# Zero-padded query blocks as stationary operand of the low-part score products in a forgetting attention

## The chip, the cores and the metric

The kernel runs on one core of one Trainium2 chip as a single launch. The metric is the device time of that core in microseconds (us). A profiled execution leaves a trace, whose times count from the first instruction of the span. TensorE (PE) multiplies matrices and has a queue of its own for loading stationary operands (PEld); VectorE is DVE, ScalarE is ACT, GpSimd is POOL, and SyncE (SP) issues DMAs.

## The reference

Two transformer blocks run one after the other on a sequence of 1024 tokens of width 1024, all in float32. The change touches only the attention of the first block, which has 8 heads of dimension 64:

```
logit[t,s] = q_t . k_s / sqrt(64) + c[t] - c[s]      c = cumsum(log_sigmoid(f)),  s <= t
p = softmax(logit);   out = p @ v
```

It is swept in blocks of 128 queries, so a head has 8 query blocks, and block i needs (i+1)*128 keys. Around it stand a gated spatial unit, the output projection and a gated feed-forward layer; the second block has a windowed attention of 16 heads, a convolution and 16 experts.

## The kernel before

**Precision.** TensorE takes fp32r operands. To come close to float32, each operand is split into a high part (the value rounded to fp32r) and a low part (the rest), and a product is the sum of high*high, high*low and low*high. A head has only 64 rows to contract, so for its scores two of these products share one matmul: `stack_q` (line 575) writes for each head a tile of 128 partitions in which one half holds the high part of q and the other half its low part. For the even head of a pair the high part is in partitions 0 to 63, for the odd head in 64 to 127. `stack_k` (line 590) writes for each head a tile with the high part of k in both halves. One matmul over 128 partitions then gives high*high plus low*high. The third product, high q with low k, is a second matmul. The low parts of both heads of a pair share one tile `kl`, even head in partitions 0 to 63 and odd head in 64 to 127, so this second matmul contracts over 64 partitions only (line 688).

**The steps.** `steps` (line 664) lists the 64 pairs (head, query block). In the steady part they come in the order (m-1,3), (m-1,2), (m,7), (m,6), (m-1,1), (m-1,0), (m,5), (m,4). Blocks 4 to 7 are the big ones. A big step's scores fill a PSUM tile `sb` of two banks, a small one's a tile `ss` of one bank; there is one buffer of each (`psp`, line 639).

**The stages of a step.** `score_mm` (S) makes the scores: per chunk of up to 512 keys the stacked product (L685), on the diagonal block also an identity times the causal mask (L687), and the low product (L688). `score_max` (M, L698, DVE) adds the keys' c, scales and takes the maximum. `score_exp` (E, L706, ACT) makes the exponentials. `probs_T` (T, L721, PE) transposes them in 128x128 blocks. `probs_H` (H, L727, ACT) and `probs_L` (L, L731, DVE) split them into high and low parts. `pvmm` (V, L740 and L741, PE) multiplies with v for two steps at once; `pv_out` (O) adds the two halves of its result, on DVE (L752) or on POOL (L756). `pair_sum` and `pair_mul` (L764, L771, L773) apply the softmax sums.

**The order** is written by hand. Every engine runs its queue in program order. `ORDB` (line 638) lists what iteration n of the main loop (line 802) emits and with what delay: V(n-6), L(n-4), T(n-3), O(n-6), the pair's normalisation, S(n), H(n-3), M(n), E(n-1). So on PE an iteration is V, T, S; on DVE L, O, M; on ACT O, H, E; on POOL the additions of O and the copies of `pair_sum`.

**The second block's attention** makes its scores with `score_mm2` (lines 1402 to 1415). It has the same stacked queries, but its low keys `kl` carry zeros in partitions 64 to 127 (L1322), so all four of its score matmuls contract over 128 partitions.

Of the kernel before, what the change touches and what calls it, by code (L numbers as in the profile page):

```python
# [9 lines left out]
F32R = mybir.dt.float32r  # L10
# [8 lines left out]
P = 128  # L19
# [3 lines left out]
def fused(tc, x, mix_norm_g, w_in, b_f, sgu_ln_g, sgu_ln_b, w_s, b_s, out_norm_g, w_out,  # L23
# [13 lines left out]
    ACT, DVE, POOL, PE = nc.scalar, nc.vector, nc.gpsimd, nc.tensor  # L37
    act = nc.scalar.activation
    ES = ExitStack()
    L, R = "left", "right"  # L40

    def pool(es, name, bufs=1, side=L, space=None):
        kw = dict(name=name, bufs=bufs)
        if space is not None:
            kw["space"] = space
        else:
            kw["side"] = side
        return es.enter_context(tc.tile_pool(**kw))
# [4 lines left out]
    def rd(ap):  # L53
        return ap.bitcast(F32)

    def split(h, l, src, scale=None):
        if scale is None:
            act(h, src, AF.Copy)  # L58
            DVE.tensor_tensor(l, src, rd(h), op=OP.subtract)  # L59
        else:  # L60
            act(h, src, AF.Copy, scale=scale)
            DVE.scalar_tensor_tensor(l, src, scale, rd(h), op0=OP.mult, op1=OP.subtract)
# [101 lines left out]
    def wsrc(w, k0, kc, c0, n):  # L164
        return w[k0 * P:(k0 + kc) * P, c0:c0 + n].rearrange("(k p) n -> p k n", p=P)
# [151 lines left out]
    for src in (mix_norm_g, out_norm_g, ffn_norm_g, norm1_g_2, norm2_g_2, conv_w_2, b_mod_2, c_2, c_ctx_2):  # L317
        n = 1
# [166 lines left out]
    for g4 in range(2):  # L485
# [3 lines left out]
        o = slice(g4 * 4, g4 * 4 + 4)  # L489
# [84 lines left out]
    qk = []  # L574
# [60 lines left out]
    es_b = ExitStack()  # L635
# [4 lines left out]
    pst = pool(es_b, "pst", 4, space=PSUM)  # L640
    ps1 = pool(es_b, "ps1", 1, space=PSUM)
    pvs = pool(es_b, "pvs", 2, R)
    pol = pool(es_b, "pol", 3, R)
    psm = pool(es_b, "psm", 3, R)
    ppt = pool(es_b, "ppt", 2, R)
    ptn = pool(es_b, "ptn", 2, R)
# [5 lines left out]
    def prep(j):  # L652
        vs[j] = pvs.tile([P, NT, 2, P], F32R, name="vhl")
        h, l = vs[j][:, :, :, :64], vs[j][:, :, :, 64:]
        vv = vraw[:, :, j * P:(j + 1) * P].rearrange("p t (o d) -> p t o d", o=2)
        for o in range(2):
            if 2 * j + o not in cns:
                cn_load(2 * j + o)
        return [
            lambda: act(h, vv, AF.Copy),  # L660
            lambda: DVE.tensor_tensor(l, vv, rd(h), op=OP.subtract),
        ]

    steps = []
# [5 lines left out]
                steps += [(m, 7 - a), (m, 6 - a)]  # L670
    live, half, pts = {}, {}, {}

    def score_mm(n):
        h, i = steps[n]
        q, k, l = qk[h]
        r = slice(64 * (h % 2), 64 * (h % 2) + 64)
        nk = (i + 1) * P
        blk = slice(i * P, i * P + P)
        if i > 3:
            sp = psp.tile([P, T], F32, name="sb", bufs=1)  # L680
        else:
            sp = psp.tile([P, 512], F32, name="ss", bufs=1)
        for c0 in range(0, nk, 512):
            cs = slice(c0, min(c0 + 512, nk))
            PE.matmul(sp[:, cs], q[:, blk], k[:, cs], start=True, stop=False)  # L685
            if c0 + 512 >= nk:
                PE.matmul(sp[:, blk], idR, cmR, start=False, stop=False)  # L687
            PE.matmul(sp[:, cs], q[r, blk], l[r, cs], start=False, stop=True)  # L688
        live[n] = sp

    def score_max(n):
# [85 lines left out]
    def done(n, d):  # L777
        h, i = steps[n]
        if i == 0 and h % 2 and h < 7:
            for x, f in zip((FS[0], last + FS[1], last + FS[2], last + FS[3]),  # L780
                            (lambda j: pair_sum(j, 0), lambda j: pair_mul(j, 0), lambda j: pair_sum(j, 1), lambda j: pair_mul(j, 1))):
                if d == x:
                    f(h // 2)
        if (h, i) == (7, 0) and d == dict(ORDB)["E"] + 1:
            DVE.reciprocal(rinv, tns[3][:, 1].rearrange("p i o -> p (i o)"))
            rx[3] = sq.rearrange("p (i o d) -> p i (o d)", o=2, d=64)
            todo.append(lambda: DVE.tensor_copy(rx[3].rearrange("p i (o d) -> p (i o) d", o=2),
                                                rinv[:, :, None].to_broadcast([P, 16, 64])))
# [7 lines left out]
    def stage(f, n):  # L796
        if 0 <= n < N:
            f(n)

    ASQ = max(steps.index((5, 0)) + last + FS[3], steps.index((7, 7))) + 1  # L800
    table = dict(S=score_mm, M=score_max, E=score_exp, T=probs_T, H=probs_H, L=probs_L, V=even(pvmm), O=even(pv_out))
    for n in range(N + last + 1):
        if n < N and steps[n] in ((0, 7), (2, 7), (4, 7), (6, 7)):
            oT.append((pq if oT else po0).tile([P, T], F32, name="qk"))
        for c, d in ORDB:
            if c == "F":
                for d in range(last + 8):
                    stage(lambda m: done(m, d), n - d)
            else:
                stage(table[c], n - d)  # L810
        if n < N and steps[n][1] == 5 and steps[n][0] in (1, 3, 5):
            todo.extend(prep(steps[n][0] // 2 + 1))
        if n < N and steps[n] == (6, 7):

            r4, r5, rw, h4, l4, wh0, wl0 = [pq.tile([P, T], F32 if i < 3 else F32R, name="qk") for i in range(7)]
            k2 = lambda a: a[:, :768].rearrange("p (k n) -> p k n", k=2)
            nc.sync.dma_start(r4, d_sgu[0])
            nc.sync.dma_start(k2(rw), wsrc(w_out, 4, 2, 0, 384))
            nc.sync.dma_start(r5, d_sgu[1])
            todo.extend([lambda: split(h4, l4, r4), lambda: split(k2(wh0), k2(wl0), k2(rw))])  # L820
        if n < N and steps[n] == (7, 7):
            h5, l5, sqs, sq = [pq.tile([P, T], F32R if i < 2 else F32, name="qk") for i in range(4)]
            todo.append(lambda: split(h5, l5, r5))

            def attn_sq(j):
                act(sq if j else sqs, oT[j], AF.Square)
                if j:
                    POOL.tensor_tensor(sqs, sqs, sq, op=OP.add)

            todo.extend([lambda j=j: attn_sq(j) for j in range(2)])  # L830
        if n == ASQ:
            todo.append(lambda: attn_sq(2))
        if todo and n >= 2:
            todo.popleft()()
# [17 lines left out]
    for i in range(NPART):  # L852
        n = -(-(FF - f0) // (NPART - i))
# [53 lines left out]
    for k in (6, 7):  # L907
# [4 lines left out]
                stage=2, scols=1536, pcols=768, name="w2")  # L912
# [456 lines left out]
    es_b = ExitStack()  # L1369
# [408 lines left out]
    for r in range(P // 8):  # L1778
        o = slice(8 * r, 8 * r + 8)
# [123 lines left out]
    for t in range(NT + 2):  # L1903
# [10 lines left out]
        if u >= 0:  # L1914
            r = rso[:, u:u + 1]
# [66 lines left out]
```

## Time and profile before

| | |
|---|---|
| runs (us) | 3078.14, 3086.30, 3086.57 |
| median (us) | 3086.3 |
| profiled execution (us) | 3078.3 |
| its span (us) | 3076.5 |
| mean granted TensorE clock, of full speed | 0.982 |
| PE busy | 2946.9 us, 96% of the span |
| DVE busy | 1730.7 us, 56% |
| ACT busy | 1350.4 us, 44% |
| POOL busy | 350.8 us, 11% |

The first block's attention runs from 254 to 414 us of the span, the second block's from 1920 to 2218 us. The ends of matmuls are modelled in the trace, and a matmul's duration overlaps the next one's. What a matmul takes of TensorE's time is therefore read from one start to the next, not from its duration.

### The profile page before, as it was taken

What the parts mean: (1) busy time and instruction counts of PE and PEld (TensorE: products, weight loads), DVE (VectorE), ACT (ScalarE), POOL (GpSimd) and SP (SyncE); (2) the same over time, 40 slices, a digit from 0 to 9 for tenths busy, and PEclk for the clock granted to TensorE, in tenths of its full rate; (3) what the DMA queues carried; (4) which work ended last, traced back from release to release, by engine and by line L of the source; (5) the groups of instructions that cost most, each with busy time, mean ns of one, the idle gap of its engine ahead of it and who ended that gap; (6) DMA issues with size and microseconds to landing.
All of it is one profiled execution on the core that took longest, in us unless ns stands there. A gap on an engine that the chain in (4) does not pass through costs nothing.

```text
span 3076.5 us, 36785 instructions
## 1 busy us (share of the span) xinstructions
PE 2946.9 (96%) x14183; PEld 2442.4 (79%) x14183; DVE 1730.7 (56%) x2485; ACT 1350.4 (44%) x2107; POOL 350.8 (11%) x301
## 2 busy tenths in 40 slices
PE   9999999999999999999999999788899879999996
PEld 7987778888888888788888888677778768888885
DVE  4345763645354445833311123787842479999998
ACT  5345753212111212422121111788821368888886
POOL 2200122000000001200000012111121301111112
PEclk9999999999999999999999999999999889999998
DMA  5120140323222222321122221000153589999997
GB/s 195 44 74 14 40 139 26 108 72 98 67 99 84 92 79 65 126 60 42 55 69 76 89 83 35 1 21 15 44 199 136 178 304 368 377 371 378 377 377 278
DMA packets 287903, 411.88 MB, mean 134 GB/s; under 512 B 13244, under 2 KB 141984, under 8 KB 287728
## 3 DMA queue, kind: packets, MB, share of 16 engines
q1 hardware_dynamic: 275744, 371.34, 34.9%
q0 software_dynamic: 10496, 37.14, 3.9%
q8 instruction: 111, 1.82, 0.3%
q10 hardware_dynamic: 1488, 1.06, 0.2%
q14 instruction: 64, 0.52, 0.1%
HBM read 365.94 MB, written 43.55 MB: 133 GB/s over the span
## 4 chain that ended last, share of the span: by engine, by line
PE 82%; DVE 6%; ACT 5%; issue 3%; DMA 3%; POOL 1%; SPq 0%; POOLq 0%; DVEq 0%; ACTq 0%
PE b L65 24%; PE b L67 24%; PE b L66 24%; ACT sm L1432 1%; ACT ph L1454 1%; PE pt L721 1%; PE b L1823 1%; PE sb L688 1%; PE po L740 1%; DVE wl L59 1%; DVE pl L1462 1%; PE sb L685 1%; PE po L741 1%; DVE sm L1425 1%; PE pt L1444 0%
## 5 line engine op out<-in xcount | busy, mean ns | idle before, releaser
L59 DVE TENSOR_TENSOR wl<-wst,wh 128x1024 fp32r<-128x1024 f32 (+2 forms) x560 | 661.4, 1211 | 452.1 <-ACT wh L58 444.2
L58 ACT ACTIVATE wh<-wst 128x1024 fp32r<-128x1024 f32 (+2 forms) x560 | 578.3, 1044 | 379.7 <-PE b L66 161.1
L66 PE MATMUL b<-xn,wh 128*128 128x512 f32 x1312 | 510.7, 389 | 2.2 <-POOL xn L1185 1.3
L65 PE MATMUL b<-xn,wh 128*128 128x512 f32 x1312 | 511.7, 390 | 0.2 <-ACT xn L1187 0.2
L67 PE MATMUL b<-xn,wl 128*128 128x512 f32 x1312 | 510.8, 389 | 0.5 <-DVE wl L59 0.5
L65 PE MATMUL b<-wh,a 128*128 128x512 f32 x768 | 302.4, 394 | 0.2 <-ACT a L58 0.2
L66 PE MATMUL b<-wl,a 128*128 128x512 f32 x768 | 299.9, 390 | 0.8 <-DVE wl L59 0.8
L67 PE MATMUL b<-wh,a 128*128 128x512 f32 x768 | 299.7, 390 | 0.4 <-DVE a L59 0.4
L66 PEld LDWEIGHTS b<-xn,wh 128*128 128x128 f32 x1312 | 246.4, 188 | 53.8 <-POOL xn L1185 1.7
L67 PEld LDWEIGHTS b<-xn,wl 128*128 128x128 f32 x1312 | 246.3, 188 | 52.3 <-DVE wl L59 1.1
L65 PEld LDWEIGHTS b<-xn,wh 128*128 128x128 f32 x1312 | 246.3, 188 | 51.4 <-ACT xn L1187 0.6
L67 PEld LDWEIGHTS b<-wh,a 128*128 128x128 f32 x768 | 144.6, 188 | 31.0 <-DVE a L59 1.1
L66 PEld LDWEIGHTS b<-wl,a 128*128 128x128 f32 x768 | 144.7, 188 | 30.5 <-DVE wl L59 1.6
L65 PEld LDWEIGHTS b<-wh,a 128*128 128x128 f32 x768 | 144.8, 188 | 29.6 <-ACT a L58 0.7
L65 PE MATMUL b<-hH,wh 128*128 128x512 f32 x352 | 137.7, 391 | 0.0
L67 PE MATMUL b<-hH,wl 128*128 128x512 f32 x352 | 137.1, 389 | 0.0
L66 PE MATMUL b<-hL,wh 128*128 128x512 f32 x352 | 136.9, 389 | 0.0
L1462 DVE TENSOR_TENSOR pl<-pt,ph 128x512 fp32r<-128x512 f32 x152 | 102.1, 687 | 32.5 <-ACT ph L1454 31.5
L1865 POOL DMA_INDIRECT d_x<-b,idxT x15 | 65.8, 4387 | 469.8 <-DVE b L1859 469.8
L58 ACT ACTIVATE hH<-sg 128x512 fp32r<-128x512 f32 x44 | 27.8, 632 | 202.7 <-DVE sg L1049 202.7
L1425 DVE CUSTOM_DVE_ANT_0 sm<-sp,mk,nsk 128x640 f32<-128x640 f32 (+1 forms) x128 | 107.1, 838 | 3.8 <-PE sp L1414 2.4
L1042 ACT ACTIVATE sg<-sg 128x512 f32<-128x512 f32 x44 | 27.7, 633 | 179.6 <-DVE sg L1041 179.6
(511 smaller groups left out, 5501.7 us busy)
## 6 DMA issues: line engine op xcount, KB each, us to landing
wst<-in_w_exp_gate_dram SPq DMA_DIRECT2D x128, 512.0 KB, 10.8
wst<-in_w_exp_up_dram SPq DMA_DIRECT2D x128, 512.0 KB, 10.8
wst<-in_w_exp_down_dram SPq DMA_DIRECT2D x128, 512.0 KB, 11.1
wst<-in_w_in_dram SPq DMA_DIRECT2D x74, 512.0 KB, 3.9
mw<-in_w_mod_dram SPq DMA_DIRECT2D x48, 512.0 KB, 4.8
wst<-in_w_gate_up_dram SPq DMA_DIRECT2D x44, 512.0 KB, 4.1
wst<-in_w_down_dram SPq DMA_DIRECT2D x16, 512.0 KB, 3.8
wst<-in_w_out_dram SPq DMA_DIRECT2D x10, 512.0 KB, 4.0
```

What stands on the lines that cost most here:

```text
L58: act(h, src, AF.Copy)
L59: DVE.tensor_tensor(l, src, rd(h), op=OP.subtract)
L65: PE.matmul(ps, lh, rh, start=start, stop=False)
L66: PE.matmul(ps, lh, rl, start=False, stop=False)
L67: PE.matmul(ps, ll, rh, start=False, stop=stop)
L685: PE.matmul(sp[:, cs], q[:, blk], k[:, cs], start=True, stop=False)
L688: PE.matmul(sp[:, cs], q[r, blk], l[r, cs], start=False, stop=True)
L721: PE.transpose(pt[:, b * P:(b + 1) * P], sm[:, (k0 + b) * P:(k0 + b + 1) * P], ident)
L740: PE.matmul(po[:, c:], v, ph[:, kb, c:], start=kb == 0, stop=False)
L1425: DVE.tensor_tensor_reduce(sms[n][:, :nk], sps.pop(n)[:, 256:256 + nk], (mk if i else mk0)[:, :nk], -0.125, nsk[:, hd:hd + 1], op0=OP.add, ...
L1462: DVE.tensor_tensor(pl, pt, rd(ph), op=OP.subtract)
L1865: nc.gpsimd.indirect_dma_start(out=d_x2, out_offset=bass.IndirectOffsetOnAxis(ap=idxT[:, e:e + 1], axis=0), in_=y, in_offset=None, compute ...
```

## The change

For the low product a stationary tile of 128 partitions is made, which has the high part of the query block in the head's own 64 partitions and zeros in the other 64. There are four such tiles, by head parity and block parity. POOL zeroes their other halves once ahead of the main loop, and copies a step's query block into the head's half two steps ahead of its use (`pad_q`, emitted right behind `score_mm` in the loop). The low product then takes the padded tile against all 128 partitions of `kl`; the other head's low keys meet zeros. The pool `pol`, from which O takes its tiles `ol`, has two buffers in place of three.

```diff
-    pol = pool(es_b, "pol", 3, R)
+    pol = pool(es_b, "pol", 2, R)
...
+    pqz = pool(es_b, "pqz", 1, R)
+    qzs = [[pqz.tile([P, P], F32R, name=f"qz{c}") for c in range(2)], [pqz.tile([P, P], F32R, name=f"qz{2 + c}") for c in range(2)]]
+    for o in range(2):
+        for t in qzs[o]:
+            POOL.memset(rd(t[64 - 64 * o:128 - 64 * o, :]), 0.0)
+    pads = {}
+
+    def pad_q(n):
+        h, i = steps[n]
+        r = slice(64 * (h % 2), 64 * (h % 2) + 64)
+        qz = qzs[h % 2][i % 2]
+        POOL.tensor_copy(qz[r, :], rd(qk[h][0][r, i * P:i * P + P]))
+        pads[n] = qz
+
+    pad_q(0)
+    pad_q(1)
+
     def score_mm(n):
         h, i = steps[n]
         q, k, l = qk[h]
-        r = slice(64 * (h % 2), 64 * (h % 2) + 64)
+        qz = pads.pop(n)
...
             PE.matmul(sp[:, cs], q[:, blk], k[:, cs], start=True, stop=False)
             if c0 + 512 >= nk:
                 PE.matmul(sp[:, blk], idR, cmR, start=False, stop=False)
-            PE.matmul(sp[:, cs], q[r, blk], l[r, cs], start=False, stop=True)
+            PE.matmul(sp[:, cs], qz, l[:, cs], start=False, stop=True)
...
             else:
                 stage(table[c], n - d)
+            if c == "S":
+                stage(pad_q, n + 2)
```

## Rows read from the trace of the kernel before

**Rows 1.** Chain of waits from 254 to 414 us: what ended last, by line.
```profile
by line: PE pt L721 23.5%; PE sb L688 14.5%; PE po L740 14.0%; PE sb L685 12.0%; PE po L741 11.4%; PE ss L688 7.0%; PE ss L685 3.3%; DVE sb L698 3.0%; issue 2.6%; PE pt L771 1.6%; PE ss L687 1.5%; PE sb L687 1.4%; DVE lb L731 1.2%; ACT qk L
```
**Rows 2.** Windows: length, busy time and count by engine, granted clock, DMA share, GB/s.
```profile
254.00:274.00 20.00, 15.68 (x49) 10.19 (x47) 9.79 (x18) 10.23 (x19) 0.00 (x0) 0.66 0.00 0
274.00:407.00 133.00, 131.93 (x804) 101.27 (x802) 99.59 (x234) 105.31 (x253) 20.16 (x27) 1.00 0.09 32
```
**Rows 3.** TensorE in order of time, first attention: start us, duration us, engine, line.
```profile
321.23 0.98 PE L721 MATMUL pt<-ident,sb 128*128 128x128 f32 x7
321.97 0.47 PE L685 MATMUL sb<-qk 128*128 128x512 f32 x1
322.37 0.50 PE L688 MATMUL sb<-qk 64*128 64x512 f32 x1
322.80 0.39 PE L685 MATMUL sb<-qk 128*128 128x256 f32 x1
323.02 0.22 PE L687 MATMUL sb<-cmR,idR 128*128 128x128 f32 x1
323.18 0.38 PE L688 MATMUL sb<-qk 64*128 64x256 f32 x1
323.49 0.38 PE L740 MATMUL po<-hs,vhl 128*128 128x256 f32 x1
323.71 0.28 PE L741 MATMUL po<-ls,vhl 128*128 128x256 f32 x1
323.83 0.28 PE L740 MATMUL po<-hs,vhl 128*128 128x256 f32 x1
...
324.30 0.22 PE L740 MATMUL po<-hs,vhl 128*128 128x128 f32 x1
324.36 0.28 PE L741 MATMUL po<-ls,vhl 128*128 128x128 f32 x1
```
**Rows 4.** The same view in the second block's attention.
```profile
2100.40 0.48 PE L1474 MATMUL po<-ph,vhl 128*128 128x512 f32 x1
2100.72 0.40 PE L1475 MATMUL po<-pl,vhl 128*128 128x512 f32 x1
2100.95 0.28 PE L1411 MATMUL sp<-kh,qs 128*128 128x256 f32 x1
2101.07 0.28 PE L1412 MATMUL sp<-kl,qs 128*128 128x256 f32 x1
2101.19 0.34 PE L1413 MATMUL sp<-kh,qs 128*128 128x384 f32 x1
```
**Rows 5.** Windows in the second block's attention; columns as in Rows 2.
```profile
2000.00:2200.00 200.00, 172.94 (x1085) 147.21 (x1084) 161.09 (x339) 177.26 (x408) 25.45 (x33) 0.97 0.05 17
2006.00:2008.00 2.00, 0.69 (x5) 0.45 (x4) 2.00 (x5) 1.94 (x6) 0.22 (x1) 0.93 0.00 0
2008.00:2010.00 2.00, 2.00 (x7) 1.71 (x8) 1.29 (x3) 1.95 (x5) 0.51 (x1) 0.50 0.03 8
```
**Rows 6.** DVE in order of time: the maxima of three big steps.
```profile
257.99 1.22 DVE L698 CUSTOM_DVE_ANT_0 sb<-sb,wst 128x1024 f32<-128x1024 f32 x1
...
333.31 1.22 DVE L698 CUSTOM_DVE_ANT_0 sb<-sb,wst 128x1024 f32<-128x1024 f32 x1 [0.87 <-issue]
...
342.48 0.96 DVE L698 CUSTOM_DVE_ANT_0 sb<-sb,wst 128x768 f32<-128x768 f32 x1 [0.76 <-PE sb L688]
```
**Rows 7.** POOL's groups: busy us, mean ns, idle before by releaser.
```profile
L756 POOL TENSOR_TENSOR qk<-qk,ol 64x256 f32<-64x256 f32 x14 | 11.7, 834 | 173.4 <-ACT ol L755 164.0 <-ACT hs L727 9.4
...
L1322 POOL MEMSET kl<- 64x1280 f32 x2 | 2.3, 1162 | 0.1
...
L611 POOL CAST idR<-ident 128x128 fp32r<-128x128 f32 x1 | 0.3, 301 | 0.0
```
**Rows 8.** TensorE in order of time at the first attention's start.
```profile
254.16 0.40 PE L67 MATMUL b<-xtH,wl 128*128 128x512 f32 x1
...
254.73 0.50 PE L688 MATMUL sb<-qk 64*128 64x512 f32 x1
...
259.27 0.49 PE L685 MATMUL sb<-qk 128*128 128x512 f32 x1 [3.13 <-DVE tn L698]
```

## The prediction

> **What bounds the kernel now.** I first read the chain of waits over the first block's attention, 254 to 414 us of the span [rows 1]: the chain lies on TensorE, and the low score product, L688, holds 14.5% and 7.0% of it, 34 of 160 us. The windows say the same [rows 2]: from 274 to 407 us PE is busy 131.93 of 133 us at full clock, ACT 105.31, DVE 99.59, POOL 20.16. So in these 133 us TensorE sets the pace, and ACT, the next, could end 28 us sooner. From 254 to 274 us it is different: PE is busy 15.68 of 20 us, at a granted clock of 0.66.
>
> Then I read PE in order of time, from start to start, since durations overlap [rows 3]. The reader is to see three kinds of step. Among products of 128 partitions, 256 columns take 0.12 us (L741 to L740, 323.71 to 323.83) and 128 columns take 0.06 (L740 to L741, 324.30 to 324.36); 512 columns take 0.23 (L1475 to L1411, [rows 4]). Behind the product of 64 partitions the next one starts late: 512 columns take 0.43 (322.37 to 322.80), 256 take 0.31 (323.18 to 323.49). And ahead of it too: L687 with 128 columns takes 0.16 until L688 starts (323.02 to 323.18). The second attention makes the same low product with 128 partitions, and there L1412 takes 0.12 for 256 columns, before it and behind it nothing is late [rows 4].
>
> **The change part by part.** *The low product.* There are 96 of them, 12 for each head (two chunks for each of the blocks 4 to 7, one for each of the others). Each keeps its columns; only its height changes.
> - Behind it: 0.43 - 0.23 = 0.20 at 512 columns and 0.31 - 0.12 = 0.19 at 256. 96 x 0.20 = 19.2 us.
> - Ahead of it: in 64 cases L687 stands there, 0.16 - 0.06 = 0.10; I take 0.09, as the trace has 0.14 to 0.16, so 5.8 us. In 32 it is a 512-column L685, which takes 0.40 (321.97 to 322.37) in place of 0.23. But that L685 follows transposes, and in the second attention the first product behind transposes takes 0.32 (L1474, 2100.40 to 2100.72) without any change of height. So 0.09 of it stays, and 32 x 0.08 = 2.6 us go.
> - One product further on: the first one behind L688 is itself slow, L740 0.22 (323.49 to 323.71) and L685 with 256 columns 0.22 (322.80 to 323.02), in place of 0.12. This is so in 61 cases (29 before an L740, 32 before a second chunk), 6.1 us.
>
> Together 33.7 us of TensorE's time, 0.35 per product. The bounds: nothing, if the lateness comes from something other than the height, and 40 us if the transposes behind 33 of the products also lose 0.2 each. I take 33.7, which rests on the nearest rows.
>
> The Trainium skill has a rule that bears on this: TensorEngine Tiling (Array Packing), Key Properties, says that a change of the tiling mode, not just of the tile, drains TensorE; 64 rows are such a mode. It names no time; the 0.20 us behind each product and the lateness ahead agree with it. Against it speaks another page of the Trainium skill, TensorE: Matmul & The Clock Gate, section Why this matters for your kernels: one matmul that contracts over 32 rows takes as long as one over 128, and a gain comes only from several at once. By that alone padding gains nothing, which is what the third rival comes to; the rows' 0.43 and 0.23 don't agree with it, unless something else makes the difference.
>
> *The copies.* 64 copies of 64x128 to fp32r on POOL. The nearest row is a cast of 128x128, 0.30 us [rows 7]; half of it is the lower bound. 64 x 0.30 = 19 us on an engine that is busy 20 of 133. A copy is queued two steps ahead, behind the score product that last read the same tile; two steps will last about 3.5 us, and what may stand ahead of it on POOL is an addition of 0.83 us [rows 7] that waits for ACT. So the copy is hidden and I cost it at nothing; what waits behind it on POOL are later additions, for which the next iterations leave time. If that cover were gone, a step would wait 0.30 us, 19 us in all.
>
> *The zeroing.* A memset of 1280 columns took 1.16 us [rows 7], so one of 128 lies between 0.12 and 0.30, taken at 0.2: four, and two copies, are 1.4 us. If they must wait for the projection's last product (254.16 + 0.40, [rows 8]), the first L688 moves from 254.73 to about 256.0, and its step ends before 257.3. The maximum of that step starts only at 257.99 [rows 6], since DVE still evacuates keys, and PE waits for it until 259.27 [rows 8]. So nothing is lost; without that cover it would be 1.3 us.
>
> *`pol` with two buffers.* Its tile `ol` is used once in two steps and read within a microsecond by an addition. Nothing, between -0.5 and 2 us.
>
> *What is late next.* There is one buffer for a big step's scores, so of two big steps in a row the second's scores wait for the first's maximum: 1.22 + 0.1 us for 1024 columns and 0.96 + 0.1 for 768 [rows 6], with about 0.2 for the two hand-overs. In that time PE has, for blocks 7 and 6, V of blocks 1 and 0 (two products of 256 columns and two of 128, 0.36) and four transposes at 0.74/7 = 0.11 [rows 3], 0.8 us, in every other head four transposes more, 1.24: it will wait 0.7 or 0.26. For blocks 5 and 4 it has V of blocks 3 and 2 (0.84) and two transposes, 1.04 of 1.24, and waits 0.2. A pair of heads so gets 0.7 + 0.26 + 2 x 0.2 = 1.36 us of waiting. The 133 us hold 86 of the 96 low products, 3.6 pairs of heads, so 4.9 us, of which 133 - 131.93 = 1.07 are there already.
>
> *The sum.* PE then needs 131.93 - 86 x 0.35 + 3.8 = 105.6 us, and ACT needs 105.31. Two engines of the same load, and DVE close behind, don't overlap fully. In the second attention, which stands like this, the busiest engine, ACT, is busy 177.26 of 200 us, 88.6% [rows 5]; the first attention has 99% now. At 88.6% the stretch takes 119 us (14 less), at 99% 106.6 (26 less). I take the middle, 93.8%: 112.5 us, 20.5 less. The other 10 low products lie mostly before 274 us, where PE also waits for DVE: between 0 and 3.5 us, taken at 1.5. The sum is -22 us. Behind the attention everything moves forward unchanged.
>
> The profiled execution took 3078.3 us (span 3076.5). The runs' median, 3086.3, is 8 us above it; of four executions two lie at either level, and no row tells why. I put the forecast between the levels: 3082.3 - 22 = 3060 us.
>
> **Rivals.**
> 1. *The gain is handed on.* ACT, DVE and PE wait for each other as in the second attention, and PE, now with gaps, falls to half clock at times, as there at 2008 us after a window with 0.69 of 2 us busy [rows 5]. -14 + 2 for such stretches, -12: 3070 us. For it: single buffers for scores, fewer than the second attention has. Against: PE can run almost two iterations ahead of ACT.
> 2. *All of it arrives.* ACT, busy 79% now, is filled to 99%, and the start gains 3.5: -30, 3052 us. Against it: PE's waits worked out above.
> 3. *The change doesn't do what it says.* The lateness comes from the order of products into one PSUM tile and not from the height. Then only a little of POOL is added: 3082 us. For it: L685 to L687 is late too, with no change of height between them. Against it: the second attention's L1412.
> 4. *Slower, by the clock.* PE, busy 99% now, gets waits, and its clock falls from 2.4 to 1.2 GHz for long, as at the attention's start, where it is 0.66 over 20 us [rows 2]. A microsecond at half clock costs 0.5; the 22 us are used up at 44 us of the stretch's 112, and with 62 the time is 3091. Against it: the second attention with PE busy 172.94 of 200 has a mean clock of 0.97 [rows 5].
>
> **How the numbers follow.** The forecast (-16 to -28 us) 0.50, rival 1 0.22, rival 2 0.08, rival 3 0.12, rival 4 0.08. About 0.3%, 9 us, is what a measurement of this kernel can tell from no change. Faster: the forecast, rival 2 and nearly all of rival 1, 0.78; within: rival 3 and the rest, 0.14; slower: 0.08. The range runs from the low level less 30 us, 3048, to the high level less 8 us, 3078; it leaves out rivals 3 and 4 for the most part. The likeliest case's own range is 3050 to 3070.
>
> **What would show it.** Behind the low products, now of 128 partitions, the next start comes after 0.23 us for 512 columns and 0.12 for 256; L687 takes 0.06. PE's busy share from 274 us on falls under 95%, ACT's rises from 79% to over 90%, and waits of PE for L698 appear between blocks 7 and 6. POOL shows 64 casts of at most 0.3 us and no wait of PE for them. The attention ends about 22 us sooner and all later stages keep their lengths. The prediction is wrong if the starts keep their 0.43 us, if PE waits for POOL, or if the clock of the stretch falls under 0.9.

## The result and the profile after

The changed kernel took 3057.3 us (median of four runs, 3056.6 to 3060.1), the kernel before 3085.3 (four runs, 3078.1 to 3086.6). The ratio is 0.9916, 95% interval 0.9898 to 0.9933, so 0.67 to 1.0% faster. In a second set on another occasion it was 0.9914, 0.9900 to 0.9928 (3059.2 us against 3084.2). The prediction was 3060 us, range 3048 to 3078. The traced executions took 3057.3 and 3078.3 us, 21.0 us apart; the medians of the two sets lie 28 and 25 us apart. Over all sets of this document the kernel before scattered from 3076 to 3089 us, which no trace explains.

The windows of the changed kernel, columns as in [rows 2]: the start of the attention, and the stretch from the 10th to the 95th of the 96 low products, which in the kernel before lies between 274.02 and 406.61 us.

```profile
254.00:274.00 20.00, 14.13 (x61) 11.09 (x60) 10.49 (x19) 12.02 (x23) 3.63 (x14) 0.74 0.00 0
270.00:272.00 2.00, 0.83 (x7) 0.54 (x5) 2.00 (x4) 1.34 (x4) 0.50 (x1) 1.00 0.00 0
273.06:383.71 110.65, 106.48 (x802) 98.40 (x801) 98.62 (x234) 102.06 (x248) 36.17 (x81) 1.00 0.11 38
```

The same stretch of the kernel before:

```profile
274.02:406.61 132.59, 131.52 (x803) 101.00 (x801) 99.18 (x233) 104.90 (x251) 20.16 (x27) 1.00 0.09 32
```

The stretch went from 132.59 to 110.65 us, 21.9 less. PE's busy time fell by 25.0 us with the same matmuls, and its idle time rose from 1.07 to 4.17 us. ACT and DVE did the same work in less time. The part before the stretch, from the first score product on, went from 19.62 to 17.41 us, and the part behind it stayed (7.47 and 7.54). So the attention, from the first score product to the first transposes behind it, went from 159.7 to 135.6 us, 24.1 less. Its two ends in the kernel before, and its end in the changed kernel (its start, 255.65, stands below):

```profile
254.40 0.40 PE L685 MATMUL sb<-qk 128*128 128x512 f32 x1
...
414.08 1.93 PE L771 MATMUL b<-ident,qk 128*128 128x128 f32 x8
```

```profile
391.25 1.06 PE L789 MATMUL b<-ident,qk 128*128 128x128 f32 x8
```

Of the 24.1 us the traced executions show 21.0. The changed kernel's attention starts 1.25 us later, and the rest is lost behind it, in stages whose code does not differ. The later start is scatter: in the second trace of the changed kernel (experiment 8) the attention starts at 254.62 and takes 135.06 us. What lies behind the attention took between 2658 and 2673 us over the traces of this document.

TensorE in order of time in the changed kernel, at the place that [rows 3] show; the low product is now L706, the stacked one L703, the mask L705:

```profile
341.98 0.48 PE L703 MATMUL sb<-qk 128*128 128x512 f32 x1
342.30 0.40 PE L706 MATMUL sb<-qk,qz 128*128 128x512 f32 x1
342.53 0.28 PE L703 MATMUL sb<-qk 128*128 128x256 f32 x1
342.65 0.22 PE L705 MATMUL sb<-cmR,idR 128*128 128x128 f32 x1
342.71 0.33 PE L706 MATMUL sb<-qk,qz 128*128 128x256 f32 x1
342.88 0.28 PE L758 MATMUL po<-hs,vhl 128*128 128x256 f32 x1
343.00 0.28 PE L759 MATMUL po<-ls,vhl 128*128 128x256 f32 x1
```

Read from start to start: behind the low product of 512 columns the next one now starts after 0.23 us (0.43 before), behind that of 256 columns after 0.17 (0.31 before). L705 takes 0.06 (0.16 before). The first L758 takes 0.12 (0.22 before).

POOL in the changed kernel, columns as in [rows 7]: the copies, what they waited for, and the zeroing.

```profile
L685 POOL CAST qz<-qk 64x128 fp32r<-64x128 f32 x64 | 20.7, 334 | 41.5 <-PE sb L706 36.3 <-PE ss L706 3.3
L774 POOL TENSOR_TENSOR qk<-qk,ol 64x256 f32<-64x256 f32 x14 | 10.9, 776 | 38.1 <-ACT ol L773 38.1
...
L678 POOL MEMSET qz<- 64x128 f32 x4 | 0.7, 198 | 52.1 <-PE b L67 52.0
```

The start of the attention, where PE waited for a copy:

```profile
255.65 0.40 PE L703 MATMUL sb<-qk 128*128 128x512 f32 x1
256.94 0.50 PE L706 MATMUL sb<-qk,qz 128*128 128x512 f32 x1 [0.90 <-POOL qz L685]
...
260.52 0.79 PE L703 MATMUL sb<-qk 128*128 128x512 f32 x1 [2.50 <-DVE tn L716]
```

And the waits of PE and its load queue in the changed kernel from 273 to 384 us: total us, times, longest.

```profile
PEld sb L703 <- DVE tn L716: 4.2, 11, 0.8
...
PEld ss L703 <- DVE tn L716: 2.5, 5, 1.0
...
PE sb L703 <- DVE tn L716: 1.7, 4, 0.6
...
PE ss L703 <- DVE tn L716: 1.4, 2, 0.8
...
PEld pt L739 <- ACT hs L745: 1.2, 1, 1.2
PE pt L739 <- DVE lb L749: 1.0, 1, 1.0
```

### The profile page after: what moved, and what is told of

It is laid out like the page before. It is cut to its first block, busy times and chain, and to the rows that moved or that the text cites. A ratio compares the mean times of both kernels' runs of the same rounds, so it can differ in the third digit from the quotient of the medians.

```text
span 3055.2 us, 36876 instructions
## 1 busy us (share of the span) xinstructions
PE 2918.8 (96%) x14183; PEld 2437.9 (80%) x14183; DVE 1729.4 (57%) x2485; ACT 1348.2 (44%) x2107; POOL 371.0 (12%) x369
## 4 chain that ended last, share of the span: by engine, by line
PE 82%; DVE 6%; ACT 6%; issue 3%; DMA 2%; POOL 1%; SPq 0%; POOLq 0%; DVEq 0%; ACTq 0%
PE b L65 25%; PE b L67 25%; PE b L66 25%; ACT sm L1452 1%; ACT ph L1474 1%; PE b L1843 1%; DVE wl L59 1%; PE pt L739 1%; DVE pl L1482 1%; PE pt L1464 1%; DVE sm L1445 1%; PE po L1494 1%; PE b L1685 0%; DMA ot<-d_o 0%; PE po L1495 0%
```

## The experiments

The first four ran on one chip, the next four together on another occasion, the last two together. Ratios are to the kernel before in the same set.

**1. All side parts, 64 rows.** The changed kernel with the low product over the head's 64 partitions.

```diff
-            PE.matmul(sp[:, cs], qz, l[:, cs], start=False, stop=True)
+            PE.matmul(sp[:, cs], qz[r, :], l[r, cs], start=False, stop=True)
```

> The changed kernel with all its side parts (four zeroed tiles, 64 copies on POOL, two ol buffers, the low product's stationary operand read from the padded tile), but the low product contracts over the head's 64 partitions only, as before. Theory (the height of the product is what counts): the start behind the low product comes back to 0.43 us at 512 columns and 0.31 at 256, and the time is that of the kernel before, ratio 0.998 to 1.002. Rival (it is the separate tile or the earlier availability of the operand): the starts stay at 0.23 and the ratio is 0.991, as for the changed kernel.

Measured: ratio 1.0003 (0.9995 to 1.0012), 3080.2 us. TensorE in order of time (the low product is L707, the first product with v L759):

```profile
323.77 0.49 PE L707 MATMUL sb<-qk,qz 64*128 64x512 f32 x1
324.19 0.39 PE L704 MATMUL sb<-qk 128*128 128x256 f32 x1
324.41 0.22 PE L706 MATMUL sb<-cmR,idR 128*128 128x128 f32 x1
324.56 0.38 PE L707 MATMUL sb<-qk,qz 64*128 64x256 f32 x1
324.88 0.39 PE L759 MATMUL po<-hs,vhl 128*128 128x256 f32 x1
```

The starts are back at 0.42 and 0.32 us though the operand is the padded tile. So the height is the cause, and the copies, the zeroed tiles and the two buffers of `pol` together cost nothing that can be measured at this pace. Experiment 2 asks the same at the faster one.

**2. Full height without copies.** The kernel before with the stacked query tile against all of `kl`; the product of the query's low part with the other head's low keys is left in.

```diff
-            PE.matmul(sp[:, cs], q[r, blk], l[r, cs], start=False, stop=True)
+            PE.matmul(sp[:, cs], q[:, blk], l[:, cs], start=False, stop=True)
```

> The kernel before with one edit: the low product takes the stacked query tile itself over all 128 partitions of the low keys, so that it adds a product of the query's low part with the other head's low keys, which is left in. No padded tiles and no copies on POOL, three ol buffers. Theory (height is what counts, POOL's copies are hidden): as the changed kernel within 3 us, 3054 to 3060 by its runs. Rival (the copies on POOL hold PE up, or the tile reuse does): faster than the changed kernel by 4 us or more.

Measured: ratio 0.9922 (0.9910 to 0.9935), 3055.1 us; the stretch took 110.67 us, the changed kernel's 110.65. The whole gain comes with the height alone, and the 64 copies are hidden. The kernel computes something slightly different: the extra term is a low part times a low part, of the size that the splitting into high and low leaves out anyway.

**3. Low products grouped.** The kernel before, both chunks' stacked products first and then both low products.

```diff
-            PE.matmul(sp[:, cs], q[r, blk], l[r, cs], start=False, stop=True)
+        for c0 in range(0, nk, 512):
+            cs = slice(c0, min(c0 + 512, nk))
+            PE.matmul(sp[:, cs], q[r, blk], l[r, cs], start=False, stop=True)
```

> The kernel before with the score products of a big step in another order: the stacked products of both chunks and the mask first, then both low products of 64 partitions. So the height changes 64 times back and forth in place of 96, with the same products. Theory (each change of height costs, not the 64 rows themselves): the first of two low products with 512 columns is followed after 0.23 us in place of 0.43; 32 times about 0.38 us of PE, 12 us, of which 8 to 12 come through: ratio 0.996 to 0.9975. Rival (a product of 64 rows is slow by itself): still 0.43 behind each low product, ratio 0.999 to 1.001.

Measured: ratio 0.9964 (0.9951 to 0.9976), 3067.8 us; the attention took 147.8 us (255.49 to 403.33), 11.8 less than before. The two low products of a big step (L690, drawn together as x2) in order of time, and below the second of them by itself:

```profile
335.04 0.59 PE L685 MATMUL sb<-qk 128*128 128x512 f32 x2
335.48 0.22 PE L687 MATMUL sb<-cmR,idR 128*128 128x128 f32 x1
335.63 0.61 PE L690 MATMUL sb<-qk 64*128 64x512 f32 x2
```

```profile
335.96 0.28 PE L690 MATMUL sb<-qk 64*128 64x256 f32 x1
336.17 0.39 PE L742 MATMUL po<-hs,vhl 128*128 128x256 f32 x1
336.39 0.28 PE L743 MATMUL po<-ls,vhl 128*128 128x256 f32 x1
```

The start behind the first low product comes after 0.33 us (335.63 to 335.96), not after the 0.23 of the expectation, and the one behind the second after 0.21 in place of 0.31. Together the two take 0.54 us, where they took 0.43 + 0.31 = 0.74 with a stacked product between them. From the mask to the second product with v (335.48 to 336.39) it is 0.91 us, 0.38 more than the 0.06 + 0.23 + 0.12 + 0.12 = 0.53 of full height. The single low product in [rows 3] is late by as much in all: 0.10 ahead of it, 0.19 behind it and 0.10 one product further on. So one change of height and back costs about 0.38 us whether one or two products of 64 rows stand in it: it is the change that costs, not the 64 rows. A third fewer changes brought 11.8 us of the 24.1, 0.37 for each of the 32 that went.

**4. Steps interleaved.** The changed kernel with big and small steps in turn; the products with v of the big pairs come one iteration later.

```diff
...
-        for a in (0, 2):
-            if m > 0:
-                steps += [(m - 1, 3 - a), (m - 1, 2 - a)]
-            if m < 8:
-                steps += [(m, 7 - a), (m, 6 - a)]
+        for a in range(4):
+            if m > 0:
+                steps.append((m - 1, 3 - a))
+            if m < 8:
+                steps.append((m, 7 - a))
...
```

> The changed kernel with the steps in another order: small and big steps alternate, (m-1,3), (m,7), (m-1,2), (m,6) and so on, so that no two big steps follow each other; the products with v of the big pairs are emitted one iteration later. Theory (of two big steps in a row the second's scores wait for the first's maximum, since there is one buffer): PE's waits for the maxima, 18 us in the changed kernel, fall under 8, and the time is 4 to 8 us below the changed kernel, 3049 to 3053. Rival (ACT, busy 92.5% of the stretch, sets the pace whatever the order): within 2 us of the changed kernel.

Measured: ratio 0.9935 (0.9922 to 0.9948), 3058.6 us; the stretch took 113.32 us, 2.7 more than in the changed kernel; as the order is another, its ends fall on other steps, but the whole attention too took 138.8 us against 135.6. PE's waits for maxima fell from 9.8 to 3.7 us between 273 and 384 us (from 18.2 to 12.2 over the whole attention, not under 8), but others came, on DVE and PE (L790 and L738 are the multiplication by the softmax sums and the transposes):

```profile
DVE qk L790 <- POOL qk L773: 6.0, 3, 4.0
...
PE pt L738 <- DVE lb L748: 2.8, 3, 1.6
...
PE pt L738 <- DVE qk L790: 1.7, 1, 1.7
...
PEld sb L702 <- DVE tn L715: 1.6, 4, 0.7
```

My theory, that the order of the steps would give 4 to 8 us, fell.

**5. Interleaved, no copies.** Experiment 4 with the operand of experiment 2, to take POOL's queue out of it.

```diff
-            PE.matmul(sp[:, cs], qz, l[:, cs], start=False, stop=True)
+            PE.matmul(sp[:, cs], q[:, blk], l[:, cs], start=False, stop=True)
...
-            if c == "S":
-                stage(pad_q, n + 2)
```

> The interleaved steps without POOL's copies: the low product takes the stacked query tile over all 128 partitions (the other head's part is left in), three ol buffers. In the interleaved kernel with copies PE waited less for maxima, but 6 us were waited by DVE for additions that stand on POOL behind copies. Theory (POOL's queue order took the gain of interleaving): 4 to 8 us below the changed kernel on this chip, 3049 to 3054. Rival (the order itself gains nothing, ACT, DVE and PE are balanced at over 90%): within 2 us of the changed kernel.

Measured: ratio 0.9929 (0.9915 to 0.9942), 3062.9 us, not below the changed kernel (3059.2 in this set). Its traced stretch took 116.25 us, at a mean clock of 0.97. PE waited for banks of the transposes, and DVE waited as long for POOL's additions as in experiment 4:

```profile
DVE qk L772 <- POOL qk L755: 6.0, 3, 3.9
...
PE pt L720 <- DVE lb L730: 2.9, 3, 1.7
```

So the copies in POOL's queue were not what took the gain: the 6.0 us are waited without them too.

**6. Less work for ACT.** The changed kernel without the exponentials of the left half of the keys, the first block apart.

```diff
-        act(sm[:, :nk], sm[:, :nk], AF.Exp, bias=mx, scale=-1.0, accum_out=sums)
+        c0 = nk // 2 if i else 0
+        act(sm[:, c0:nk], sm[:, c0:nk], AF.Exp, bias=mx, scale=-1.0, accum_out=sums)
```

> The changed kernel with the exponentials of the left half of the keys left out for all blocks but the first, which takes some 14 to 16 us of work off ACT alone. Theory (ACT, busy 92.5% of the stretch, sets the pace now): the stretch of 86 low products, 110.65 us, falls by 6 to 10 us, since PE's 102 us are then the bound, and the time by as much. Rival (the hand-overs between PE and DVE set it): under 3 us.

**7. Less work for DVE.** The changed kernel without the low parts of the probabilities from the fifth key block on.

```diff
-        for hv, lv, v in half.pop(n):
+        for hv, lv, v in half.pop(n)[:1]:
...
-            PE.matmul(po[:, c:], v, pl[:, kb, c:], start=False, stop=kb == i + 1)
+            PE.matmul(po[:, c:], v, (pl if kb < 4 else ph)[:, kb, c:], start=False, stop=kb == i + 1)
```

> The changed kernel with the low parts of the probabilities left out beyond the fourth key block (the high part stands in their place, so PE does the same), which takes some 16 us of work off DVE alone. Theory (ACT sets the pace): under 3 us less. Rival (DVE, busy 88.6%, sets it because the maxima wait behind its other work): 5 to 10 us less, and PE's waits for the maxima halve.

Measured: ratio 0.9912 (0.9896 to 0.9928), 3055.4 us, without half the exponentials; 0.9910 (0.9895 to 0.9925), 3054.9 us, without the low parts. The medians lie 3.8 and 4.3 us under the changed kernel's of this set, and the intervals overlap with its interval. The windows of the stretch, first less ACT, then less DVE:

```profile
271.06:380.36 109.30, 105.91 (x802) 98.19 (x801) 98.38 (x234) 90.45 (x250) 36.65 (x81) 1.00 0.12 39
```

```profile
270.87:380.78 109.91, 106.35 (x803) 98.64 (x801) 88.56 (x205) 101.54 (x247) 36.14 (x81) 1.00 0.12 38
```

ACT lost 11.6 us of work and the stretch 1.35; DVE lost 10.1 and the stretch 0.7. PE is busy 106 us in both. Neither ACT nor DVE sets the pace by its load; PE's own work fills 96.9 and 96.8% of the stretch. So the theory of experiment 6 fell, and its rival's number came. The theory of experiment 7 gave the right number, but its reason, ACT, did not hold; its rival fell, and PE's waits for maxima did not halve (10.3 us by the wait rows from 273 to 384 us, 9.8 in the changed kernel). Less work was taken off than the expectations say.

**8. The changed kernel again**, unedited, in the set of 5 to 7.

> The changed kernel once more, unedited, beside the others on one chip. Whatever the theory: ratio 0.991 to 0.994 to the kernel before. If its time differs from that of the version without copies by less than 3 us, the copies are hidden; if it is 4 us or more above, they aren't.

Measured: ratio 0.9914 (0.9900 to 0.9928), 3059.2 us; its stretch took 110.72 us, its attention 135.06. The copies cost nothing here either: the version without them had 0.9922, in another set. The start of its attention:

```profile
254.62:271.41 16.79, 10.65 (x48) 8.21 (x46) 9.54 (x17) 10.38 (x20) 3.63 (x13) 0.80 0.00 0
```

**9. Two buffers for big scores**, paid for with two banks of the transposes.

```diff
-    pst = pool(es_b, "pst", 4, space=PSUM)
+    pst = pool(es_b, "pst", 2, space=PSUM)
...
-            sp = psp.tile([P, T], F32, name="sb", bufs=1)
+            sp = psp.tile([P, T], F32, name="sb", bufs=2)
```

> The changed kernel with two PSUM buffers for the scores of a big step in place of one, and two banks in place of four for the transposed probabilities. Relieving ACT by about 10 us moved the stretch by 1.4 us and relieving DVE by 9 us by 0.8, so I now hold that PE's own work and its waits for the maxima fill the stretch. Theory: the waits of sb for the maximum, 5.9 us in the stretch, vanish, and the time falls by 3 to 6 us, unless the transposes now wait for their banks. Rival (the banks for transposes are what lets PE run ahead): waits of L739 for L749 of more than 6 us, the time equal or up to 15 us longer.

**10. Two buffers for small scores**, paid for with one bank of the transposes.

```diff
-    pst = pool(es_b, "pst", 4, space=PSUM)
+    pst = pool(es_b, "pst", 3, space=PSUM)
...
-            sp = psp.tile([P, 512], F32, name="ss", bufs=1)
+            sp = psp.tile([P, 512], F32, name="ss", bufs=2)
```

> The changed kernel with two PSUM buffers for the scores of a small step in place of one, and three banks in place of four for the transposed probabilities. Theory: the waits of ss for the maximum, 4 us in the stretch, vanish, the time falls by 1 to 4 us. Rival as above: the transposes wait instead, and the time is equal or up to 8 us longer.

Measured: with two big buffers ratio 1.0076 (1.0057 to 1.0094), 3105.4 us; with two small ones 0.9996 (0.9985 to 1.0006), 3079.5 us. The waits of PE from 273 to 400 us, with two big buffers:

```profile
PEld pt L739 <- issue: 29.9, 26, 2.9
...
PE pt L739 <- DVE lb L749: 29.7, 23, 2.8
```

and with two small ones:

```profile
PEld pt L739 <- PE pt L739: 12.8, 13, 1.1
...
PE pt L739 <- DVE lb L749: 11.1, 14, 1.2
```

The waits for sb's and ss's maxima went or shrank, and far more was waited for the banks of the transposes. The rival held both times, with a larger loss than it had put down: by the ratios some 50 and 25 us over the changed kernel, in place of at most 15 and 8. These banks let PE run ahead, and giving up one of them took the whole gain of the change. Two things came on top. The clock granted in the stretch fell to a mean of 0.95 and 0.97. And with two big buffers the first score product started 4.7 us late, after a wait for ACT. Whether the waits for maxima would come through as time with banks to spare is open, since each edit takes from the transposes what it gives to the scores.

## Why the prediction came out

- **Where the time was.** Right. The lateness around the low product was due to its height (experiments 1 to 3), about 0.38 us for a change and back. This agrees with the rule of the Trainium skill that a change of tiling mode drains TensorE (TensorEngine Tiling (Array Packing), Key Properties); that it is a drain which takes the time, no run here shows. The other rule of the Trainium skill that the prediction cites, that few rows take as long as many (TensorE: Matmul & The Clock Gate, Why this matters for your kernels), agrees only where no change of height comes in: in experiment 3 the second low product adds 0.54 - 0.31 = 0.23 us for 512 columns, as at 128 rows.
- **Its size.** 0.35 us per product were put down, 30.1 us for the stretch's 86; PE's busy time fell by 25.0, 0.29 per product. The term that was too large is the one behind the product: 0.20 was taken everywhere. In the changed kernel it is 0.20 where another score product follows (0.43 to 0.23), but 0.14 where a product with v (0.31 to 0.17) or a transpose follows (0.37 to 0.23 at 384 columns; the rows of the changed kernel stand in the last section):

```profile
311.68 0.44 PE L688 MATMUL ss<-qk 64*128 64x384 f32 x1
312.05 0.77 PE L721 MATMUL pt<-ident,sb 128*128 128x128 f32 x5
```

  The latter two hold for 58 of the 86 products, and 58 x 0.06 = 3.5 us of the 5.1. The sign that the prediction gave for 256 columns, 0.12 us to the next start, was missed with it, and so was PE's busy share under 95% (it is 96.2).
- **The copies and the zeroing.** Right in what they cost: 334 ns each in place of at most 300, hidden but for one wait of 0.90 us at the start. That wait lies in the time that PE waits for the first maximum anyway, which ends 4.87 us behind the first score product in both kernels (254.40 to 259.27, 255.65 to 260.52). The prediction called any wait of PE for POOL a sign that it is wrong; this one cost nothing.
- **What is late next.** Waits for maxima came, but only in part where they were worked out. PE's own rows put its idle time down to the maxima of big steps (1.7 us), those of small steps (1.4) and the low parts of probabilities (1.0). The prediction had 4.9 us at big steps and none elsewhere. 6.7 us more stand on the load queue for the maxima of both kinds. That PE's idle time rose by 3.1 us in place of 3.8 is near for a sum whose parts are other ones.
- **The sum's last step** gave the right number for a reason that didn't hold, and that was luck. It took PE and ACT as two engines of equal load at 93.8%, which made 112.5 us of the 105.6 that PE was to need. The stretch took 110.65: the first terms were about 5 us short, and the 6.9 us of this step covered that. Experiments 6 and 7 show that the load of ACT or DVE is not what holds the stretch: with ACT at 83% it moved by 1.35 us. What the trace leaves is PE's own account, work and waiting: 132.59 - 25.0 + 3.1 = 110.7 us.
- **The start.** 2.2 us gained, 1.5 put down; the clock had a part in it that the prediction did not have. Over the 20 us its mean was 0.66 in the kernel before and is 0.74 now. With two levels, 1.2 and 2.4 GHz, that means about 13.6 us at the lower one before and 10.4 now. In the second trace of the changed kernel (experiment 8) it was about 6.7 us, and the same part took 16.79 us in place of 17.41. So the clock differs from one execution to the next, and how much of the 2.2 us it gave is not shown.
- **The rivals.** The third fell with experiment 1, and the fourth with the clock, 1.00 in the stretch. The second, 106.6 us for the stretch, is PE's 106.48 us of work with hardly a wait, and it fell by the 4.17 us of waiting. The first had the right idea, hand-overs, but they took only 3 us more than before, and no half clock came with them.

## What to carry to other kernels

Where products over 64 and over 128 partitions alternate on TensorE, look at the distance from start to start around each; group those of one height, or fill the shorter ones up to full height, which cost no time here (0.23 us for 512 columns). Before a tile is zero-padded for that, see whether the full stacked operand does: here it gave the same time without copies, at the price of an extra product of low parts in the result (experiment 2). Before a buffer is taken from one stage for another, see which waits it holds back.

## What the runs showed of the hardware

- A product of 64 rows between products of 128 rows starts about 0.09 us late itself, the next starts 0.14 to 0.20 us later than it would, and the one behind that 0.10. Two products of 64 rows in a row pay that once and not twice (0.54 us in place of 0.74, experiment 3).
- Behind the last score product of a step 0.05 us remain even at full height. From its start to that of the transposes, a product of 384 columns takes 0.23 us in the changed kernel's first attention and 0.18 in the second attention of the kernel before. The cause was not followed up. In order of time, the first attention and then the second:

```profile
333.70 0.39 PE L706 MATMUL ss<-qk,qz 128*128 128x384 f32 x1
333.93 0.71 PE L739 MATMUL pt<-ident,sb 128*128 128x128 f32 x5
```

```profile
2101.36 0.34 PE L1414 MATMUL sp<-kl,qs 128*128 128x384 f32 x1
2101.54 0.38 PE L1444 MATMUL pt<-ident,sm 128*128 128x128 f32 x2
```

- POOL's cast of 64 partitions took 334 ns, that of 128 partitions 301 [rows 7], both with 128 columns: half the partitions did not shorten it.
